# Tile 0 of x goes unscaled into plain fp32 products; its roots multiply the sums, its forms are scaled afterwards

## The chip, the core and the metric

The kernel runs on one core of a Trainium2 chip. Five engines matter here: TensorE (PE in the profile, its weight loads PEld), VectorE (DVE), ScalarE (ACT), GpSimd (POOL), and SyncE (SP), which issues most loads; POOL issues the DMAs that add to what lies at their target. The metric is the time of one execution in microseconds (us), as the median of several runs.

## What is computed

One layer of a hybrid encoder block on x of 1024 tokens by 1024 features. What the change touches is the norm at the start, and the projection of its result by the columns of `w_in` that give `vs`, the input of the gating branch:

```python
def rmsnorm(x, g):
    xf = x.astype(jnp.float32)
    y = xf * lax.rsqrt(jnp.mean(xf * xf, axis=-1, keepdims=True) + EPS)
    return (y * g.astype(jnp.float32)).astype(x.dtype)
...
        h = rmsnorm(x, norm_g[l])
        proj = h @ w_in[l]
        q, k, v, za, u, vs, zs, gm = jnp.split(proj, IN_SPLITS, axis=-1)
```

The root of a token is a factor on its whole row, so it can be multiplied in before the product or after it; g is a factor on each feature and has to be there before. Attention, the other projections, the gating and the final norm follow and are not changed.

## The kernel before, in words

**Products.** A product of 1024x1024 by 1024x1024 is done by 2x2 blocks of 512 in seven block products rather than eight (Strassen's scheme in Winograd's form). The forms of h that go into the seven are named `b11, t1, t2, b21, t3, b22, t4`, those of the weight `a11, s1, s2, a12, s3, s4, a22`. Each operand is split into a high part in fp32r (a cast on ACT) and the rest (a subtraction on DVE), and a block product is three fp32r products: high by high, high by low, low by high. So a tile of 128 tokens costs, for one block product, 4 chunks of 128 features by 3 terms, 12 matmuls of 128x128 by 128x512.

**The first stage** makes `vs`, token tile by token tile, while x is still coming in. SP issues loads of 512 KB in this order: x tile 0, the two halves of a11, x tile 1, the two halves of a12, x tile 2, the two halves of s1's first block, g spread over 128 partitions, x tiles 3 and 4, and, as buffers come free, x tiles 5, 6, 7. For each x tile, `scale_of` (L616) squares and sums the rows on ACT and makes the root in five small steps on DVE and one on ACT; `turned_half` (L626) multiplies half a tile by root and g on DVE (L629) and turns it on PE in four transposes into a PSUM bank named `ps_sc` (L634), of which there are two. Tiles 0 to 3 are the first token half: `first_tile` (L654) makes the high and low parts of b11 and b21 from the banks and keeps the raw values in `xh`, and `first_product` (L763) makes the block products by a11 (`accs[t]`) and by a12 (`m2`, stored in `xh` by ACT). Tiles 4 to 7 are the second token half: `second_tile` (L668) subtracts from the kept raw values of tile t-4, and makes the forms t1 and b22, from the same two banks. `by_s1` and `by_s4` then make the block products of t1 and b22, four tiles each; those of tiles 2 and 3 use the `ps_sc` banks too. The products by s2 on the form t2 follow, and from there on the stage and the rest of the kernel keep their order under the change.

**The order.** The engines' queues are filled at build by a scheduler that goes by its own estimates. `after(second, first)` forbids only that the second comes earlier than the first on its engine; it does not place it. An engine's queue is worked through in the order in which it was filled.

**The start.** Before the first x tile is there, PE multiplies ones by ones (`keep_busy`, 12 matmuls), and g, split in two parts in partition 0 of `g_both`, is spread over the 128 partitions by a product with ones into two banks (`spread`, L573), from which tiles 0 and 1 are scaled.

## Time and profile before

| | us |
|---|---|
| median of 3 runs | 901.23 |
| lowest and highest run | 900.76, 901.72 |
| the profiled execution, whole | 901.17 |
| its span, first to last instruction | 899.4 |
| PE busy in the span | 889.1 |
| granted TensorE clock, mean | 0.998 |

1.77 us of the profiled execution lie outside its span. Times within the trace count from the span's start. In a timeline row stand the start, the length up to the end of the last of the merged instructions, the engine, the line, what it writes and reads, and in square brackets the idle time before it and what ended it. PE's matmuls overlap: one of 512 columns lasts 0.39 us, and the next starts 0.227 us after it. Names lose their numbers in the profile: `ps_sc` is any of the two banks, `wr` any x tile in its landing buffer, `T_t1h` the high part of form t1.

### The profile page before, as it was taken

The page shows a single profiled execution, that of the slowest core. Times are in us where ns is not written, and L with a number is a line of the kernel's source. Part 1 is how long each engine was busy: PE and PEld are TensorE (multiplying, and loading weights), DVE is VectorE, ACT ScalarE, POOL GpSimd, SP SyncE. Part 2 cuts the span into 40 slices and gives each one's busy share as a digit, 9 for nine tenths or more (in the row PEclk, how much of TensorE's full clock was granted, in tenths as well). Part 3 has the DMA queues.
Part 4 walks back from the last instruction along what each step waited for, and adds up shares of the span by engine and source line. Part 5 has one row for each costly group of instructions (what it writes and reads, how often), then busy time and mean ns, then how long its engine had stood idle before and what let it go on. Part 6 is the DMA issues. An engine that isn't in the chain of part 4 may idle for free.

```text
span 899.4 us, 13233 instructions
## 1 busy us (share of the span) xinstructions
PE 889.1 (99%) x4304; PEld 743.7 (83%) x4304; DVE 685.8 (76%) x1251; ACT 532.0 (59%) x1064; POOL 149.8 (17%) x213
## 2 busy tenths in 40 slices
PE   8999999999999999999999999999999999999997
PEld 6788888888888888888888888888888888888885
DVE  7879966666687788888878888646796488479986
ACT  7875533334455567676777776755585376467453
POOL 2322222203030001111210111100121121110012
PEclk9999999999999999999999999999999999999999
DMA  9997888868778767878787788899899789998533
GB/s 327 215 258 218 263 208 175 165 157 260 259 253 284 214 188 213 216 151 214 178 221 227 248 241 194 232 316 365 308 284 376 288 226 259 301 301 282 186 116 118
DMA packets 132750, 213.77 MB, mean 238 GB/s; under 512 B 12777, under 2 KB 61161, under 8 KB 132682
## 3 DMA queue, kind: packets, MB, share of 16 engines
q1 hardware_dynamic: 110072, 149.74, 49.9%
q0 software_dynamic: 22464, 62.93, 31.4%
q8 instruction: 34, 0.56, 0.2%
q14 instruction: 34, 0.28, 0.1%
q10 hardware_dynamic: 146, 0.27, 0.1%
HBM read 147.74 MB, written 86.11 MB: 260 GB/s over the span
## 4 chain that ended last, share of the span: by engine, by line
PE 97%; DMA 1%; ACT 1%; DVE 0%; issue 0%; SPq 0%
PE ps_mm L353 42%; PE ps_o L353 27%; PE ps_tp L353 7%; PE ps_sc L1341 3%; PE ps_sc L353 3%; PE ps_tp L750 2%; PE ps_o L1428 2%; PE ps_tp L1387 2%; PE ps_mm L750 2%; PE ps_o L750 2%; PE ps_tp L1012 2%; PE ps_sc L750 1%; PE ps_sc L634 1%; DMA T_t3h<-in_w_dram 1%; ACT wh L162 0%
## 5 line engine op out<-in xcount | busy, mean ns | idle before, releaser
L162 ACT CAST wh<-s 128x1024 fp32r<-128x1024 f32 (+1 forms) x79 | 79.3, 1006 | 92.8 <-PE ps_mm L353 42.4
L163 DVE TENSOR_TENSOR wl<-wr,wh 128x512 fp32r<-128x512 f32 (+1 forms) x77 | 72.0, 936 | 53.2 <-ACT wh L162 52.6
L163 DVE TENSOR_TENSOR wl<-s,wh 128x1024 fp32r<-128x1024 f32 (+1 forms) x79 | 92.6, 1172 | 11.0 <-ACT wh L162 10.9
L162 ACT CAST wh<-wr 128x512 fp32r<-128x512 f32 (+1 forms) x77 | 63.1, 820 | 59.6 <-PE ps_mm L353 30.5
L353 PE MATMUL ps_o<-T_t1h,wh 128*128 128x512 f32 x148 | 58.6, 396 | 0.0
L353 PE MATMUL ps_o<-T_t1h,wl 128*128 128x512 f32 x148 | 57.7, 390 | 0.0
L353 PE MATMUL ps_o<-T_t1l,wh 128*128 128x512 f32 x148 | 57.6, 389 | 0.0
L1356 ACT ACTIVATE pr<-ps_sc,sm 128x192 f32<-128x192 f32 (+2 forms) x128 | 50.9, 410 | 7.4 <-DVE sm L1350 6.4
L353 PE MATMUL ps_mm<-T_t3h,wh 128*128 128x512 f32 x140 | 54.9, 392 | 0.0
L353 PE MATMUL ps_mm<-T_b11h,wh 128*128 128x512 f32 x140 | 54.9, 392 | 0.0
L353 PE MATMUL ps_mm<-T_b11l,wh 128*128 128x512 f32 x140 | 54.7, 391 | 0.0
L353 PE MATMUL ps_mm<-T_t3h,wl 128*128 128x512 f32 x140 | 54.7, 390 | 0.0
L353 PE MATMUL ps_mm<-T_b11h,wl 128*128 128x512 f32 x140 | 54.7, 390 | 0.0
L353 PE MATMUL ps_mm<-T_t2h,wl 128*128 128x512 f32 x140 | 54.6, 390 | 0.0
L353 PE MATMUL ps_mm<-T_t2h,wh 128*128 128x512 f32 x140 | 54.6, 390 | 0.0
L353 PE MATMUL ps_mm<-T_t2l,wh 128*128 128x512 f32 x140 | 54.5, 390 | 0.0
L353 PE MATMUL ps_mm<-T_t3l,wh 128*128 128x512 f32 x140 | 54.5, 389 | 0.0
L353 PE MATMUL ps_mm<-T_t4h,wh 128*128 128x512 f32 x136 | 53.6, 394 | 0.0
L353 PE MATMUL ps_mm<-T_t4h,wl 128*128 128x512 f32 x136 | 53.2, 391 | 0.0
L353 PE MATMUL ps_mm<-T_t4l,wh 128*128 128x512 f32 x136 | 52.9, 389 | 0.0
L307 POOL DMA_DIRECT2D sums<-in_w_dram x40 | 29.8, 939 | 91.6 <-ACT x L371 42.2
L353 PE MATMUL ps_o<-T_b22h,wh 128*128 128x512 f32 x108 | 42.7, 395 | 0.0
(420 smaller groups left out, 2448.2 us busy)
## 6 DMA issues: line engine op xcount, KB each, us to landing
wr<-in_w_dram SPq DMA_DIRECT2D x86, 256.0 KB
sums<-in_w_dram POOLq DMA_DIRECT2D x20, 512.0 KB, 7.0
s<-sums SPq DMA_DIRECT2D x20, 512.0 KB
q_hl<-qhl SPq DMA_DIRECT2D x16, 512.0 KB
q<-q_hl SPq DMA_DIRECT2D x64, 128.0 KB
y_dr<-x POOLq DMA_DIRECT2D x28, 256.0 KB, 6.7
g<-in_w_dram POOLq DMA_DIRECT2D x12, 512.0 KB, 6.6
wr<-in_w_dram SPq DMA_DIRECT2D x11, 512.0 KB
```

The lines of the kernel that those rows point to most:

```text
L162: hi_of.append(nc.scalar.copy(hi, src))
L163: return nc.vector.tensor_sub(lo, src, hi.bitcast(F32))
L307: return lambda: paced(nc.gpsimd.dma_start(dst, src, accum_op=op))
L353: nc.tensor.matmul(acc, lt, rt, start=fresh and k == 0 and n == 0, stop=k == 3 and n == 2, skip_group_check=True,)
L634: turns.append(nc.tensor.transpose(pt[:, i * P : (i + 1) * P], xt[:, k * P : (k + 1) * P], ident[:]))
L750: mm = nc.tensor.matmul(acc[:], lt, rt, start=fresh and k == 0 and n == 0, stop=k == 3 and n == terms[-1], skip_group_check=True,)
L1012: nc.tensor.matmul(pm[:, t * P : (t + 1) * P], xh[:, half * 4 + t, g * P : (g + 1) * P], bias[-1][1][:, g % 4, :], start=True, stop=True,)
L1341: nc.tensor.matmul(sc[:, i, k0:], q_of[:, c, i * P : (i + 1) * P], kt[:, f, k0:], start=f == 0, stop=f == 1,)
L1356: nc.scalar.activation(held_in[c, i], sc[:, i, lo:hi], AF.Exp, bias=nmax[:, c, i : i + 1], scale=-1.0, accum_out=sums[:, c, i : i + 1],)
L1387: nc.tensor.transpose(dst, pr[:, i, block * P : block * P + width], ident[:])
L1428: nc.tensor.matmul(po[:, cs], lt, rt, start=n == 0, stop=n == len(terms) - 1)
```

## The change

Tile 0 is turned as it lands, without root or g (`turn_unscaled`); DVE multiplies by g on the way from the bank to `xh`, with g as one column for each chunk of features (`g_col`, made by eight turns of one row on PE). Its two block products go as plain fp32 matmuls, unsplit, 4 and 4, straight on the raw weights that have landed (`unscaled_product`); ACT multiplies both sums by the root (the products end in `accs[0]` and `m2` as before). The forms b11 and b21 of tile 0, which later stages need, are made afterwards: the root is put on a diagonal, a product with ones spreads it across (`spread_root`, one fp32 matmul of 128x128 by 128x128), DVE multiplies the raw values by it, and they are split as before (`scale_unscaled`). The keep-busy matmuls go from 12 to 6. The spread of g moves in between the products of tile 0. Tile 1's products take the low part of b11 and b21 last. `amid` asks that the transposes of tiles 2 to 5 come no earlier than a given matmul, and the work of tile 4 stands between the two halves of the split of s1. `after.py` writes lines some 40 to 80 higher: L632 for L634, L645 for L647, L627 for L629, L792 for L750.

```diff
@@ -96,14 +96,18 @@
-    plain = mtile([P, D], F32, "wl", 3)[:, 0:HALF]
     g_row = mtile([P, D], F32, "wh", 3)[0:1, :]
     nc.scalar.dma_start(g_row, norm_g.partition_broadcast(1))
-    nc.vector.memset(plain, 1.0)
+    ones_r = mtile([P, 4, HALF], F32R, "T_b22l", 1)[:, 0, :]
+    g_both = mtile([P, 4, HALF], F32R, "T_t1h", 1)
+    nc.vector.memset(ones_r.bitcast(F32), 1.0)
     ident = const.tile([P, P], F32, name="ident")
...
     nc.gpsimd.memset(eps_sb[:], EPS)
+    g_col = const.tile([P, KC], F32, name="g_col")
+    for at, engine in ((0, nc.vector), (2, nc.gpsimd)):
+        engine.memset(g_both[:, at : at + 2, :].bitcast(F32), 0.0)
     warm = const.tile([P, 1], F32, name="warm")
...
@@ -540,9 +544,6 @@
-    ones_r = slot("b22l", (P, HALF))
-    ones_made = nc.vector.tensor_copy(ones_r[:], plain)
     fed = []
...
@@ -552,15 +553,11 @@
         for _ in range(n):
-            feed(nc.tensor.matmul(idle[:], ones_r[:, 0:P], ones_r[:], start=True, stop=True))
+            feed(nc.tensor.matmul(idle[:], ones_r[:, 0:P], ones_r, start=True, stop=True))
...
     g_in = [bank("tp") for half in range(2)]
-    g_both = slot("t1h")
     g_parts = [g_both[:, 2 * n : 2 * n + 2, :] for n in range(2)]
-    for half in range(2):
-        after(nc.vector.memset(g_parts[0][:, half, :].bitcast(F32), 0.0), ones_made)
-    nc.gpsimd.memset(g_parts[1].bitcast(F32), 0.0)
     for half in range(2):
...
@@ -573,11 +570,12 @@
-    keep_busy(4)
-    for n in range(2):
-        for half in range(2):
-            spread(n, half)
-    keep_busy(8)
+    keep_busy(5)
+    g_turned = bank("o")
+    for k in range(KC):
+        feed(nc.tensor.transpose(g_turned[:, k : k + 1], g_row[:, k * P : (k + 1) * P], ident[0:1, 0:1]))
+    g_kept = nc.scalar.copy(g_col[:], g_turned[:, 0:KC])
+    keep_busy(1)
...
@@ -620,10 +618,10 @@
-            after(square, casts[2 * t - 3])
+            after(square, casts[2 * t - 5])
         return xt, rstd_of(ss[:], 1.0 / D)
...
-    def turned_half(xt, r, j):
+    def turned_half(xt, r, j, t=None):
         cs = half_of(j)
...
@@ -632,8 +630,8 @@
             turns.append(nc.tensor.transpose(pt[:, i * P : (i + 1) * P], xt[:, k * P : (k + 1) * P], ident[:]))
-            if len(turns) == 1:
-                feed(turns[0])
+            if t == 1:
+                feed(turns[-1])
         return pt
...
@@ -651,19 +649,63 @@
-    def first_tile(t, scale=None):
-        xt, r = scale or scale_of(t)
-        left = []
-        for j, name in enumerate(("b11", "b21")):
-            pt = turned_half(xt, r, j)
-            form_of(name, t, by_k(pt[:]))
-            if j:
-                left.append(lambda pt=pt: nc.scalar.mul(raw_b21(t), pt[:], -1.0))
-            else:
-                left.append(lambda pt=pt: nc.scalar.copy(raw_sum(t), pt[:]))
-            if t:
-                left.pop()()
-        return left
+    def first_half(t, j, xt, r):
+        name = ("b11", "b21")[j]
+        pt = turned_half(xt, r, j, t)
+        form_of(name, t, by_k(pt[:]))
+        if j:
+            return lambda: nc.scalar.mul(raw_b21(t), pt[:], -1.0)
+        return lambda: nc.scalar.copy(raw_sum(t), pt[:])
+    def first_tile(t):
+        xt, r = scale_of(t)
+        for j in range(2):
+            first_half(t, j, xt, r)()
+    def unscaled(j):
+        return by_k((raw_sum, raw_b21)[j](0))
+    def turn_unscaled(j):
+        pt = bank("sc")
+        for i in range(4):
+            k = j * 4 + i
+            feed(nc.tensor.transpose(pt[:, i * P : (i + 1) * P], x_in[0][:, k * P : (k + 1) * P], ident[:]))
+        return nc.vector.tensor_mul(
+            unscaled(j), by_k(pt[:]), g_col[:, 4 * j : 4 * j + 4].unsqueeze(2).broadcast_to([P, 4, P])
+        )
+    def unscaled_product(acc, j, *ks):
+        for k in ks:
+            feed(
+                nc.tensor.matmul(
+                    acc[:],
+                    unscaled(j)[:, k, :],
+                    raws[("a11", "a12")[j]][:, k, :],
+                    start=k == 0,
+                    stop=k == 3,
+                    skip_group_check=True,
+                )
+            )
+    def spread_root(r):
+        diagonal, across = (x_place(1, 1, 0)[:, i * P : (i + 1) * P] for i in range(2))
+        nc.scalar.mul(diagonal, ident[:], r[:])
+        summed = bank("sc")[:, 0:P]
+        nc.tensor.matmul(summed, ones_r[:, 0:P].bitcast(F32), diagonal, start=True, stop=True)
+        nc.scalar.copy(across, summed)
+        return across.unsqueeze(1).broadcast_to([P, 4, P])
+    def scale_unscaled(j, across, late=None):
+        hi, lo = (v[:, :, tokens(0)] for v in hb[("b11", "b21")[j]])
+        raw = unscaled(j)
+        if j:
+            after(nc.vector.scalar_tensor_tensor(raw, raw, -1.0, across, op0=ALU.mult, op1=ALU.mult), late)
+        else:
+            nc.vector.tensor_mul(raw, raw, across)
+        split(hi, lo, raw, j == 1)
...
@@ -755,17 +797,27 @@
                     )
+                    steps.append(mm)
         return mm
...
     accs = {}
+    steps = []
     t5s = {}
+    def amid(t, half, product, n):
+        turn, step = turns[8 * (t - 1) + 4 * half], steps[24 * (product - 1) + n]
+        after(turn, step)
...
         accs[t] = bank("mm" if t < 2 else "tp")
-        terms = (0, 1, 2) if t else (0, 2, 1)
-        vs_product(accs[t], "b11", t, "a11", True, terms=terms)
         m2 = bank("o")
-        vs_product(m2, "b21", t, "a12", True, terms=terms)
+        for acc, name, weight in ((accs[t], "b11", "a11"), (m2, "b21", "a12")):
+            if t == 1:
+                vs_product(acc, name, t, weight, True, terms=(0, 1))
+                vs_product(acc, name, t, weight, False, terms=(2,))
+            else:
+                vs_product(acc, name, t, weight, True)
         nc.scalar.copy(x_place(0, 0, t), m2[:])
...
@@ -783,25 +835,28 @@
-    first = scale_of(0)
     for name, at in (("a11", "t3h"), ("a12", "t3l")):
...
     first_lows = []
+    _, root = scale_of(0)
+    after(squares[0], g_kept)
+    turned = [turn_unscaled(j) for j in range(2)]
+    after(of_mean[0], turned[1])
     split_vs(0)
+    after(first_lows[0], turned[1])
+    accs[0] = bank("mm")
+    unscaled_product(accs[0], 0, 0, 1)
+    for n in range(2):
+        for half in range(2):
+            spread(n, half)
+    unscaled_product(accs[0], 0, 2, 3)
+    split_vs(1)
     second = scale_of(1)
-    unsplit = first_tile(0, first)
-    after(of_mean[1], lows[0])
-    after(first_lows[0], scalings[1])
-    after(lows[0], first_lows[0])
-    split_vs(1)
-    after(first_lows[2], lows[0])
-    after(lows[1], first_lows[2])
-    after(casts[0], hi_of[0])
-    after(squares[1], casts[0])
-    after(casts[1], squares[1])
+    after(squares[1], hi_of[0])
+    after(of_mean[1], first_lows[2])
     for c in (2, 3):
...
@@ -814,11 +869,21 @@
         x_in[t] = load_x(t)
-    for c in (2, 3):
-        split_vs(c)
-        after(first_lows[c + 1], lows[1])
-        after(hi_of[c - 1], casts[1])
-    for move in unsplit:
+    m2 = bank("o")
+    split_vs(2)
+    after(hi_of[1], of_root[1])
+    unscaled_product(m2, 1, 0, 1, 2)
+    split_vs(3)
+    left = [first_half(1, 0, *second)]
+    unscaled_product(m2, 1, 3)
+    left.append(first_half(1, 1, *second))
+    after(hi_of[2], hi_of[1])
+    after(first_lows[3], scalings[1])
+    after(first_lows[4], first_lows[3])
+    after(lows[0], first_lows[4])
+    m2_kept = nc.scalar.mul(x_place(0, 0, 0), m2[:], root[:])
+    after(nc.scalar.mul(accs[0][:], accs[0][:], root[:]), casts[1])
+    for move in left:
         move()
...
@@ -827,23 +892,40 @@
     raws["s2"], raws["s4"] = raws["a11"], raws["a12"]
-    first_tile(1, second)
-    after(scalings[2], first_lows[4])
+    first_tile(2)
+    after(of_mean[2], lows[0])
+    after(lows[1], scalings[3])
+    after(squares[2], hi_of[2])
+    after(casts[0], squares[2])
+    after(of_root[2], casts[0])
+    after(casts[1], of_root[2])
+    after(m2_kept, casts[1])
     g_of[:] = [g_sb[:, half, :] for half in range(2)]
-    first_tile(2)
-    first_product(0)
     first_tile(3)
+    after(of_mean[3], lows[1])
     first_product(1)
+    amid(2, 0, 1, 11)
+    amid(2, 1, 1, 15)
+    across = spread_root(root)
+    scale_unscaled(0, across)
     s1_hl = slot("t2h"), slot("t2l")
...
             vs_w["s1", 2 * c + k] = hi[:, k, :], lo[:, k, :]
-    second_tile(4)
+        if c == 0:
+            second_tile(4)
     first_product(2)
+    amid(3, 0, 2, 7)
+    amid(3, 1, 2, 13)
+    scale_unscaled(1, across, lows[-1])
     second_tile(5)
     first_product(3)
+    amid(4, 0, 3, 3)
+    amid(4, 1, 3, 9)
+    amid(5, 0, 3, 17)
+    amid(5, 1, 3, 21)
     for c in range(2):
...
```

What the scheduler makes of it, at three places. First PE's queue at the start, before (`ps_sc_196`, `ps_sc_204`: tile 0 turned; `ps_mm_296`: its product by a11):

```order
L555 MATMUL ps_sc_123<-T_b22l_121 128x512 x8
L634 MATMUL ps_sc_196<-ident,wr_119 128x128 x4
L634 MATMUL ps_sc_204<-ident,wr_119 128x128 x4
L750 MATMUL ps_mm_296<-wh_177,T_b11h_150 128x512 x2
L750 MATMUL ps_mm_296<-wh_177,T_b11l_151 128x512 x2
L750 MATMUL ps_mm_296<-wl_178,T_b11h_150 128x512 x2
L750 MATMUL ps_mm_296<-wh_211,T_b11h_150 128x512 x2
L750 MATMUL ps_mm_296<-wh_211,T_b11l_151 128x512 x2
L750 MATMUL ps_mm_296<-wl_212,T_b11h_150 128x512 x2
```

and in the change (`ps_sc_175`, `ps_sc_181`: tile 0 turned; L682: the fp32 products by a11, `ps_mm_193`, and by a12, `ps_o_235`; L570: the spread of g; `ps_sc_248`, `ps_sc_257`: tile 1 turned):

```order
L673 MATMUL ps_sc_175<-ident,wr_123 128x128 x4
L673 MATMUL ps_sc_181<-ident,wr_123 128x128 x4
L682 MATMUL ps_mm_193<-T_t3h_157,xh_120 128x512 x2
L570 MATMUL ps_tp_126<-T_t1h_69,T_b22l_68 128x512
L570 MATMUL ps_tp_127<-T_t1h_69,T_b22l_68 128x512
L570 MATMUL ps_tp_126<-T_t1h_69,T_b22l_68 128x512
L570 MATMUL ps_tp_127<-T_t1h_69,T_b22l_68 128x512
L682 MATMUL ps_mm_193<-T_t3h_157,xh_120 128x512 x2
L682 MATMUL ps_o_235<-T_t3l_158,xh_120 128x512 x3
L632 MATMUL ps_sc_248<-ident,wr_161 128x128 x4
L682 MATMUL ps_o_235<-T_t3l_158,xh_120 128x512
L632 MATMUL ps_sc_257<-ident,wr_161 128x128 x4
```

Of the 24 matmuls of tile 0 there are 8, they stand behind the loads of the weights and no longer behind splits, and tile 1 is turned among them.

Second, ACT's queue around the square of x tile 3 (`wT,st<-T_t1l`), before:

```order
L663 COPY xh_116<-ps_sc_249 128x512
L661 ACTIVATE xh_116<-ps_sc_258 128x512
L619 ACTIVATE wT_154,st_61_323<-T_t1l_223 128x1024
L647 CAST T_b11h_150<-ps_sc_279 128x4x128
```

and in the change:

```order
L658 COPY xh_120<-ps_sc_248 128x512
L617 ACTIVATE wT_152,st_61_304<-T_t1l_226 128x1024
L657 ACTIVATE xh_120<-ps_sc_257 128x512
L645 CAST T_b11h_148<-ps_sc_287 128x4x128
```

The row L661 (L657), which empties the second bank of tile 1, stood ahead of the square of tile 3 and stands behind it now.

Third, PE's queue where tile 5 is turned (`ps_sc_463`, `ps_sc_473`, then `ps_sc_454`, `ps_sc_464`), and the first products by s1 (`ps_o_517` and `ps_o_508` of tile 4; `ps_o_572` of tile 5). Before:

```order
L750 MATMUL ps_o_495<-wh_232,T_b21l_153 128x512 x2
L634 MATMUL ps_sc_463<-ident,wr_226 128x128 x4
L634 MATMUL ps_sc_473<-ident,wr_226 128x128 x4
L750 MATMUL ps_o_495<-s_236,T_b21h_152 128x512 x2
L750 MATMUL ps_o_495<-s_237,T_b21h_152 128x512 x2
L750 MATMUL ps_o_495<-s_236,T_b21l_153 128x512 x2
L750 MATMUL ps_o_517<-T_t2h_380,T_t1h_398 128x512 x2
L750 MATMUL ps_o_517<-T_t2l_381,T_t1h_398 128x512 x2
L750 MATMUL ps_o_517<-T_t2h_380,T_t1l_399 128x512 x2
L750 MATMUL ps_o_517<-T_t2h_380,T_t1h_398 128x512 x2
L750 MATMUL ps_o_517<-T_t2l_381,T_t1h_398 128x512 x2
L750 MATMUL ps_o_517<-T_t2h_380,T_t1l_399 128x512 x2
```

In the change:

```order
L792 MATMUL ps_o_508<-T_t2l_369,T_t1h_384 128x512 x2
L792 MATMUL ps_o_508<-T_t2h_368,T_t1l_385 128x512 x2
L792 MATMUL ps_o_508<-T_t2h_368,T_t1h_384 128x512 x2
L792 MATMUL ps_o_508<-T_t2l_369,T_t1h_384 128x512 x2
L792 MATMUL ps_o_508<-T_t2h_368,T_t1l_385 128x512 x2
L632 MATMUL ps_sc_454<-ident,wr_229 128x128 x4
L632 MATMUL ps_sc_464<-ident,wr_229 128x128 x4
L792 MATMUL ps_o_572<-T_t2h_368,T_t1h_384 128x512 x2
```

And where tile 7 is turned and the third product by s1 follows, before (`ps_sc_608`, `ps_sc_618`; `ps_sc_663`):

```order
L634 MATMUL ps_sc_608<-ident,wr_230 128x128 x4
L750 MATMUL ps_o_581<-wh_509,T_b22h_400 128x512
L750 MATMUL ps_o_581<-wl_510,T_b22h_400 128x512 x2
L634 MATMUL ps_sc_618<-ident,wr_230 128x128 x4
L750 MATMUL ps_o_581<-wh_509,T_b22l_401 128x512 x2
L750 MATMUL ps_o_581<-wh_513,T_b22h_400 128x512 x2
L750 MATMUL ps_o_581<-wl_514,T_b22h_400 128x512 x2
L750 MATMUL ps_o_581<-wh_513,T_b22l_401 128x512 x2
L750 MATMUL ps_sc_663<-T_t2h_380,T_t1h_398 128x512 x2
```

and in the change (`ps_sc_599`, `ps_sc_609`; `ps_sc_654`):

```order
L792 MATMUL ps_o_572<-wh_504,T_b22l_387 128x512 x2
L632 MATMUL ps_sc_599<-ident,wr_233 128x128 x4
L632 MATMUL ps_sc_609<-ident,wr_233 128x128 x4
L792 MATMUL ps_sc_654<-T_t2h_368,T_t1h_384 128x512 x2
```

The transposes of tile 5 stood 18 matmuls ahead of the end of the first product by s1; they stand behind it now, and the next row is the product that reads tile 5. Those of tile 7 stood 11 and 8 matmuls ahead of the third product by s1, and stand right ahead of it now.

## The prediction

> **What bounds the kernel now.** I read the page first, then the chain that ended last, the waits, and the timelines of PE, ACT and DVE up to 63 us.
>
> ```profile
> span 899.4 us, 13233 instructions
> ...
> PE 889.1 (99%) x4304; PEld 743.7 (83%) x4304; DVE 685.8 (76%) x1251; ACT 532.0 (59%) x1064; POOL 149.8 (17%) x213
> ...
> PE 97%; DMA 1%; ACT 1%; DVE 0%; issue 0%; SPq 0%
> ```
>
> The chain is PE almost from end to end. The busy times by stretch (columns: stretch, its length, then PE, PEld, DVE, ACT and POOL with counts, clock, DMA share, GB/s) say where PE still has room:
>
> ```profile
> 5.60:17.50 11.90, 10.59 (x49) 7.41 (x48) 9.84 (x21) 9.84 (x19) 3.20 (x3) 1.00 1.01 398
> 17.50:62.50 45.00, 44.80 (x216) 35.94 (x217) 36.75 (x77) 33.60 (x63) 12.05 (x14) 1.00 1.04 236
> 62.50:899.40 836.90, 830.28 (x4033) 697.87 (x4031) 635.79 (x1147) 484.82 (x979) 132.82 (x188) 1.00 0.80 236
> ```
>
> And where the chain turns into PE for good:
>
> ```profile
> 1.64 6.55 DMA T_t3h<-in_w_dram
> ...
> 17.53 3.02 PE ps_mm L750 x12
> ...
> 51.79 10.88 PE ps_sc L750 x48
> ```
>
> Until 17.5 us the start runs through a load, splits, a root and scalings; from the first product of tile 1 at 17.53 on PE does not stop. So the change can win only in the first 17.5 us, while whatever it makes PE wait before 62.5 us is added in full: behind that stretch the longest wait of a weight load is 0.4 us, so nothing there takes up a delay.
>
> ```profile
> PEld ps_o L1428 <- DVE x L383: 0.4, 1, 0.4
> ```
>
> **Prices on PE.**
>
> ```profile
> 5.71 2.02 PE L555 MATMUL ps_sc<-T_b22l 128*128 128x512 f32 x8
> 7.75 1.33 PE L634 MATMUL ps_sc<-ident,wr 128*128 128x128 f32 x8
> ...
> 112.41 1.95 PE L1012 MATMUL ps_tp<-wT,xh 128*128 128x128 f32 x16
> 114.11 0.48 PE L353 MATMUL ps_mm<-T_t4h,wh 128*128 128x512 f32 x1
> ...
> L1012 PEld LDWEIGHTS ps_tp<-wT,xh x128: 187/192/192, 112.2 to 187.1; 128*128 128x128 f32 x128
> ```
>
> In the chain 48 fp32r products take 10.88 us: 0.227 each. L1012 is the only plain fp32 product shown: 8 instructions of 128 columns, two records each, hold PE from 112.41 to 114.11 at least and 1.78 at most (16 records of 0.111, the distance of the transposes). That is 0.22 for 128 columns, and four times that, 0.89, for 512. Tile 0 then costs 8 x 0.89 = 7.1 us of PE in place of 24 x 0.227 = 5.4: 1.7 more. An fp32 product of 512 columns is not in the trace; from below it is at least 4 x 0.2125 = 0.85, from above 1.27 if its two weight loads (0.19 each at L1012) stood open. I take 0.89, which scales the row without a gap. The root's product, 128 columns, is 0.22.
>
> **The start, step by step.** Loads land one behind the other, 0.524 MB at 398 GB/s, one in 1.32 us. The third, a11's second half, lands at 1.64 + 6.55 = 8.19. So x tile 1 is there at 9.5, a12 at 10.8 and 12.1, x tile 2 at 13.5, and x tile 3, the eleventh, at 18.7. The eighth should then land at 14.8, and POOL, waiting for it, starts at 14.87:
>
> ```profile
> 14.87 1.04 POOL L606 DMA_DIRECT2D T_t4h<-in_w_dram  x1 [6.34 <-DMA T_t4h<-in_w_dram]
> ...
> 24.60 0.86 POOL L606 DMA_DIRECT2D T_t3h<-T_t4h  x1 [7.58 <-DVE T_t1l L629]
> ...
> 4.50 1.06 ACT L619 ACTIVATE wT<-wr 128x1024 f32<-128x1024 f32 x1 [0.27 <-DMA wr<-in_x_dram]
> ...
> 19.40 1.05 ACT L619 ACTIVATE wT<-T_t1l 128x1024 f32<-128x1024 f32 x1
> 20.35 0.19 ACT L619 ACTIVATION_READ_ACCUMULATOR wT<-T_t1l 128x1 f32 x1
> ```
>
> x tile 0 lands at 4.5. Behind the turns of g and one keep-busy matmul its eight transposes end near 6.3; DVE multiplies both halves by g, 0.6 each, until 7.3, so PE begins the fp32 products at 7.0. Two (1.78), the four spreads (0.91), two more: 11.45. a12 is there by then; three products 14.1, half of tile 1 turned (0.44), the last product 15.45, the other half 15.9. The turns of tile 1 find their data: square at 9.5, root done at 11.9, scaled by 13.3. So the first product of tile 1 starts at **15.9 and not 17.53: 1.6 us won**, the whole of the gain. Splits of a11 and a12, still needed by tiles 1 to 3, lie beside it on ACT and DVE.
>
> **First new wait: x tile 3.** Behind the last turn of tile 1 (15.9 and 0.2 to its end) ACT has a cast, the two multiplications by the root and a copy, 0.49 each, reaches the square of tile 3 at about 18.1 and stands until 18.7, when it lands; before, ACT came there at 19.40 and found it. The square with its read holds ACT about 1.05, and only then L657 empties the bank in which tile 2's second half is to be turned: 18.73 + 1.05 + 0.6 and a step to PE = 20.55. PE is there at 15.9 + 16 x 0.227 + 0.44 = 19.95. **0.6 lost**, and from here PE's place is tied to the landing, whatever the fp32 products took within 0.6.
>
> **Second: tile 5.** From 20.55 to the end of the first product by s1 PE has 68 matmuls, 20 transposes and the root's product: 15.4 + 2.2 + 0.2 = 17.9, so it could be done at 38.4. Next are tile 5's transposes, which need it scaled by DVE.
>
> ```profile
> 29.54 1.22 DVE L652 TENSOR_TENSOR T_t2l<-T_t4h,T_t2h 128x1024 fp32r<-128x1024 f32 x1
> 30.68 0.68 DVE L674 TENSOR_TENSOR xh<-xh,ps_sc 128x512 f32<-128x512 f32 x1
> ...
> 34.83 0.16 DVE L150 TENSOR_TENSOR st<-st,st 128x1 f32<-128x1 f32 x1
> 35.02 1.41 DVE L629 SCALAR_TENSOR_TENSOR wr<-wr,st,xh 128x512 f32<-128x512 f32 x2
> 36.36 0.69 DVE L683 TENSOR_TENSOR xh<-xh,T_t4l 128x512 f32<-128x512 f32 x1
> 36.96 0.68 DVE L674 TENSOR_TENSOR xh<-xh,ps_sc 128x512 f32<-128x512 f32 x1
> ```
>
> From start to start a split of 1024 takes 1.14, a scaling 0.67, a subtraction 0.60, a small step 0.17 to 0.2. In the change tile 4's second half is turned by 32.5 (20.55, then 42 matmuls, 20 transposes and the root's product, 12.0), its cast on ACT done by 33.3, and between there and tile 5's scaling DVE has: two small steps 0.34, a subtraction 0.61, tile 0's multiplication by the root 0.67 (new), a subtraction 0.61, a small step 0.17, a subtraction 0.61, the second split of s1 1.14 (before, it stood far ahead of tile 5), tile 0's split 0.67 (new): 4.8, so 38.15. The scalings end at 38.9 and 39.55, and PE waits 0.4 for the one and 0.2 for the other, and 0.1 before that for the split. The transposes end at 40.07. The next product reads t1 of tile 5, and for this ACT does three things in its queue's order, as it does here for tile 6:
>
> ```profile
> 45.94 0.59 ACT L647 CAST T_b22h<-ps_sc 128x512 fp32r<-128x512 f32 x1 [1.08 <-PE ps_sc L634]
> 46.42 0.61 ACT L675 ACTIVATE x<-ps_sc 128x512 f32<-128x512 f32 x1
> 46.91 0.62 ACT L647 CAST T_t1h<-xh 128x512 fp32r<-128x512 f32 x1
> ```
>
> That is 0.2 to the end of the last transpose, 0.48 + 0.49 + 0.62 and a step: 1.9. Before, 18 matmuls (4.1 us) covered this trip; in the change nothing stands between. **2.6 lost at tile 5.**
>
> **Third: tile 7.** 36 matmuls and 8 transposes later (9.1 us) PE turns tile 7 right ahead of the third product by s1. That product writes the bank of tile 7's first half, so it waits for ACT's cast of the second half and then its copy of the first: 0.2 + 0.48 + 0.6 and a step, 1.36; and tile 7's scaling on DVE, queued behind the late work of tile 6, costs 0.5 more. **1.9 lost.** Before, 8 matmuls and more stood between.
>
> **The sum.** What falls away in turn are the small stalls of before in the same stretch: from 17.53 to
>
> ```profile
> 62.51 0.61 PE L750 MATMUL ps_mm<-wh,T_t2h 128*128 128x512 f32 x2
> ```
>
> are 44.98 us, of which 168 matmuls and 48 transposes make 38.1 + 5.3; 1.5 was waiting. So: -1.6 (start) + 0.6 (tile 3) + 0.2 (root's product) + 2.6 (tile 5) + 0.1 (tile 6) + 1.9 (tile 7) - 1.5 = **+2.3**. The span becomes 901.7; with the 1.77 outside it the profiled execution goes from 901.17 to 903.5, which stands to the median of 901.23 as near as nothing. Forecast **903.5**. Its own bounds: the tile 5 trip can be 0.6 shorter if DVE's scaling is in time, and DVE can be 0.8 later by its order: 902.7 to 904.4. What costs nothing here costs nothing for named reasons: the unsplit products' larger price and ACT's two multiplications by the root are covered by the wait for tile 3; and the doubled reads of a11 and a12 are over by 15.5, ahead of the POOL adds into them, which come from 24.60 on (POOL's second row above).
>
> **Rivals.**
> *The start gain stays* (the other side). If DVE and ACT finish tiles 5 and 7 ahead of PE, only -1.6 + 0.6 + 0.2 is left, and up to 1.5 of the old stalls may go too: 899 to 900.4, say 900. For it speaks that DVE is busy 36.75 of 45 us; against it that the two trips begin with transposes that end where the reader starts. It decides from the point where 4 us of other matmuls stand between, and none do. 9%.
> *One trip only.* If the bank of tile 7 comes free by the other buffer, 1.9 falls away: 901.6. 10%.
> *The clock opens late.* PE's products begin at 2.19 at some 0.45 each:
>
> ```profile
> 2.19 2.08 PE L555 MATMUL ps_sc<-T_b22l 128*128 128x512 f32 x4 [2.19 <-DVE T_b22l L544]
> ```
>
> and run at 0.23 from 5.71, 3.5 us later. The change has half the keep-busy matmuls, with transposes and a gap of 0.6 behind them. If full speed came 3.5 us later, at 9.2, two us of fp32 products would go at half speed and the transposes of tile 0 be later by 0.4: 1.5 more, 1.2 of it behind what the wait for tile 3 hides: 904.7. 13%. [...]
> *Weight loads stand open* in the fp32 products: 8 x 0.38 = 3.0, 0.6 hidden: 905.9. Against it: at L1012 they overlap. 4%.
>
> **How the numbers follow.** The forecast has 64%. A measurement here tells 0.2% from no change: below 899.4 is faster, above 903.03 slower. Of the 64, some 52 lie above 903.03; with the late clock and the open loads 69 slower. Same: 12 of the forecast, 10 for one trip, 5 of the first rival: 27. Faster: 4. The range goes from 901.8 to 905.0: it leaves out the first and the last rival and the edges.
>
> **What would show it.** After: the first product of tile 1 (L792 on `ps_mm`) at 15.9; PE idle by 0.6 near 20, freed by ACT L657; two gaps, of about 1.9 near 42 ahead of `ps_o<-T_t2h`, freed by ACT L645, and of about 1.4 near 54 ahead of `ps_sc<-T_t2h`, freed by ACT L717; the products on form t2 beginning near 64.8 and not 62.5. Wrong, if those gaps are under 1 us; if fp32 matmuls stand more than 1 us apart; or if PE's first products on a11 last twice as long.

## The result: slower, and by four times what was forecast

| | before | after |
|---|---|---|
| median of four runs, us | 901.36 | 910.27 |
| lowest and highest run | 900.76, 901.72 | 909.09, 911.64 |
| ratio, 95% interval | | 1.0100 (1.0088 to 1.0113) |
| profiled execution, whole | 901.17 | 910.05 |
| its span | 899.4 | 908.3 |

The forecast was 903.5 with a range up to 905.0. 8.9 us were added; 2.3 were forecast.

### The profile after

Of the page of the changed kernel, the span and the head of the chain that ended last:

```profile
span 908.3 us, 13224 instructions
...
PE 85%; issue 6%; DVE 3%; DMA 3%; POOL 1%; ACT 1%; POOLq 0%; DVEq 0%; ACTq 0%
```

The chain was 97% PE and is 85% PE: DMA, DVE, POOL and ACT have come into it, so PE waits somewhere where it did not. The waits of PE (line waited for, in total, times, longest) say where:

```profile
PE ps_mm L792 <- ACT wh L166: 3.3, 1, 3.3
PE ps_o L792 <- ACT T_t1h L645: 1.7, 1, 1.7
...
PE ps_sc L792 <- ACT x L717: 1.2, 1, 1.2
```

The second and third were forecast. The first, the longest, was not. PE's timeline puts it behind 70.58:

```profile
65.60 0.62 PE L792 MATMUL ps_mm<-wh,T_t2h 128*128 128x512 f32 x2
...
70.58 0.61 PE L792 MATMUL ps_tp<-wh,T_t2l 128*128 128x512 f32 x2
74.47 0.99 PE L792 MATMUL ps_mm<-wh,T_t2h 128*128 128x512 f32 x2 [3.27 <-ACT wh L166]
75.73 1.22 PE L792 MATMUL ps_mm<-wl,T_t2h 128*128 128x512 f32 x2 [0.27 <-DVE wl L167]
...
79.26 0.61 PE L792 MATMUL ps_tp<-wh,T_t2h 128*128 128x512 f32 x2
```

and the same products before:

```profile
67.94 0.61 PE L750 MATMUL ps_mm<-wh,T_t2h 128*128 128x512 f32 x2
68.40 0.62 PE L750 MATMUL ps_mm<-wl,T_t2h 128*128 128x512 f32 x2
...
70.67 0.61 PE L750 MATMUL ps_tp<-wh,T_t2h 128*128 128x512 f32 x2
```

Read the delay off such pairs. The first product on form t2 comes at 65.60 against 62.51: 3.1 late, near the forecast 2.3. The next pair is 74.47 against 67.94: 6.5. One pair on, 75.73 against 68.40: 7.3, since the low half of the weight is late as well (the row calls only 0.27 of these 0.8 a wait, because the pair ahead took 0.99 and not 0.61). At 79.26 against 70.67 it is 8.6, and the span ends 8.9 late. In the stretch between, the clock had gone down: it reads 0.50 from 75 to 78. The first of these by its row (length, then PE, PEld, DVE, ACT, POOL with counts, granted clock, DMA share, GB/s):

```profile
75.00:76.00 1.00, 0.73 (x3) 0.27 (x2) 0.80 (x2) 1.00 (x2) 0.00 (x0) 0.50 0.21 82
```

So the 8.9 are: 3.1 up to 65.6; 3.4 of standing; 0.8 for the low half; 1.3 at half clock; 0.3 later.

### Behind the stop: a DMA that landed 9.7 us later

PE waited for ACT's cast of the weight s2 (L166). ACT's timeline shows what held ACT, after:

```profile
70.54 0.59 ACT L836 COPY xh<-ps_sc 128x512 f32<-128x512 f32 x1 [6.55 <-DMA xh<-xh]
...
73.39 1.03 ACT L166 CAST wh<-T_t3h 128x1024 fp32r<-128x1024 f32 x1
```

and before:

```profile
60.85 0.59 ACT L784 COPY xh<-ps_sc 128x512 f32<-128x512 f32 x1
...
63.70 1.03 ACT L162 CAST wh<-T_t3h 128x1024 fp32r<-128x1024 f32 x1
```

The copy (`keep_t5`, the third block product by s1 put into `xh`) overwrites what one of POOL's adding DMAs, tile 6's, reads. Before, it stands there without a wait. The DMAs issued in a window of 1 us, with KB and us to landing, give this add before, and after:

```profile
xh<-xh POOLq DMA_DIRECT2D x1, 256.0 KB, 10.1
```

```profile
xh<-xh POOLq DMA_DIRECT2D x1, 256.0 KB, 19.5
```

Of POOL's issues before, those of tile 5's and tile 6's add:

```profile
41.74 0.86 POOL L606 DMA_DIRECT2D xh<-xh  x1 [0.31 <-DVE xh L683]
...
50.67 0.86 POOL L606 DMA_DIRECT2D xh<-xh  x1 [0.38 <-DVE xh L683]
```

Before, tile 6's add was issued at 50.67, so landed near 60.8: ACT's copy started at 60.85 and had at most a tenth of a us to spare. After it was issued at 50.94, hardly later, and landed at 70.44. The chain of waits of the changed kernel leads back from there (start, length, what):

```profile
44.49 2.35 DVE wl L650 x2
46.84 0.61 DVE xh L725
...
47.74 0.86 POOL xh L604
...
50.94 19.50 DMA xh<-xh
```

DVE makes tile 5's sum (L725) behind two splits of s4 now, since tile 5 is turned late; so POOL issues tile 5's add at 47.74 and no longer at 41.74, and behind it in one go two adds of 512 KB and two more of 256 KB. Just then the DMA engines ran nearly empty. The stretch 50 to 54 before, and after:

```profile
50.00:54.00 4.00, 4.00 (x19) 3.30 (x18) 3.77 (x7) 3.02 (x5) 2.01 (x3) 1.00 1.08 283
```

```profile
50.00:54.00 4.00, 3.37 (x18) 2.33 (x16) 3.20 (x8) 0.58 (x2) 2.16 (x3) 1.00 0.28 70
```

Five adds wait and the share of the DMA engines is 0.28 at 70 GB/s, not 1.08 at 283. The queues in this stretch (packets, MB, share) are, after:

```profile
DMA packets 660, 0.28 MB, mean 70 GB/s; under 512 B 574, under 2 KB 574, under 8 KB 660
...
q1 hardware_dynamic: 631, 0.23, 20.8%
q0 software_dynamic: 29, 0.05, 7.1%
```

574 packets under 512 B, nearly all of them in SP's queue, and 29 packets of the adds. By their sizes in the trace 358 of the 574 have 8 bytes, 158 have 32 or 64, and the rest 4. Which loads have such pieces is in the code: of the five small loads that SP issues behind a22, three (`ln_g`, `ln_b`, `b_merge`) fill 32 or 64 bytes of each partition, and the two of `sinks` write 2 floats, 8 bytes, at a time:

```python
    of_head = sinks.rearrange("(c e r) -> e c r", e=2, r=2)
    for e in range(2):
        behind(
            nc.sync.dma_start(
                sink_sb[e * 64 : (e + 1) * 64].rearrange("p (c r) -> p c r", r=2),
                of_head[e].partition_broadcast(64),
            ),
            mm,
        )
```

16 heads make 4 pieces in each of 128 partitions, 512 pieces in all (an expectation below says 64 x 8 for each load; it is 64 x 4). SP issued them at 44.17 after, at 45.45 before.

When the pieces were issued tells little of when they ran. By the packets' sizes they ran from 58 to 66 before, behind large loads, and from 48.7 to 55.4 after. Before, they ran beside adds whose packets were already coming, and there the two queues moved about as many packets each, 334 and 331, at a share of 1.27. The queues from 58 to 61, before:

```profile
q0 software_dynamic: 334, 0.61, 111.4%
q1 hardware_dynamic: 331, 0.01, 15.6%
```

So pieces beside adds need not cost anything. After, most of them ran when the last add's packets were through and those of the adds issued from 47.74 on had not begun. Some of the hole is only that: in the first experiment below, without the small pieces, the adds issued from 47.47 on have 2 packets between 50.5 and 51.5 as well, but large loads fill the engines. From 52 to 54 the adds have 135 packets there and 22 in the change; that is what they lose.

### The profile page after: what moved, and what is told of

It reads as the page before. It is cut to its first block, busy times and chain, and to the rows that moved or that the text cites. A ratio compares the mean times of both kernels' runs of the same rounds, so it can differ in the third digit from the quotient of the medians.

```text
span 908.3 us, 13224 instructions
## 1 busy us (share of the span) xinstructions
PE 893.5 (98%) x4300; PEld 744.3 (82%) x4300; DVE 686.4 (76%) x1251; ACT 531.9 (59%) x1066; POOL 149.5 (16%) x213
## 4 chain that ended last, share of the span: by engine, by line
PE 85%; issue 6%; DVE 3%; DMA 3%; POOL 1%; ACT 1%; POOLq 0%; DVEq 0%; ACTq 0%
PE ps_mm L357 36%; PE ps_o L357 25%; PE ps_tp L357 4%; PE ps_sc L1423 3%; PE ps_sc L357 3%; PE ps_o L1510 2%; PE ps_tp L1469 2%; DMA xh<-xh 2%; PE ps_tp L792 2%; PE ps_mm L792 2%; PE ps_tp L1094 2%; PE ps_o L792 1%; DMA bq<-bq 1%; DVE wl L167 1%; POOL y_dr L512 1%
## 5 line engine op out<-in xcount | busy, mean ns | idle before, releaser
L166 ACT CAST wh<-s 128x1024 fp32r<-128x1024 f32 (+1 forms) x79 | 79.3, 1005 | 90.7 <-PE ps_mm L357 42.6
L166 ACT CAST wh<-wr 128x512 fp32r<-128x512 f32 (+1 forms) x77 | 63.1, 820 | 58.4 <-PE ps_mm L357 30.2
```

What stands on the lines that cost most here:

```text
L166: hi_of.append(nc.scalar.copy(hi, src))
```

## The experiments

All times are medians in us, with the kernel before measured on the same chip in brackets, and the ratio's interval. Two theories of the stop at 71 were put against each other: A, the small pieces hold the adds up; B, tile 5's sum is late, whatever else the DMA engines do. None of the edits leaves out a part of the computation.

### The small loads moved away

The five small loads go behind the last product by s1:

```diff
-    behind(nc.sync.dma_start(lg_sb[:], ln_g), mm)
...
-    by_s1(3)
+    mm = by_s1(3)
+    behind(nc.sync.dma_start(lg_sb[:], ln_g), mm)
...
```

> The changed kernel, in which SP issues the five small loads (ln_g, ln_b, b_merge and the two of sinks) behind the fourth product by s1 instead of behind the first one. In the changed kernel PE stands 3.27 us from 71.2 because ACT's third copy of keep_t5 waits until 70.44 for POOL's adding DMA of tile 6 (issued at 50.94); the DMA engines are busy only a quarter of the time from 50 to 54 us, while those small loads run. Theory A, the small loads hold the DMA engines and the adds behind them: without them the add lands before 65, PE no longer stands at 71, 3.3 + 0.8 + 1.2 us (the stop, the wait for the low half of the split behind it, the slow products behind it) come back: 905 (904.5 to 906). Theory B, the adds are late because POOL issues them late and the large loads beside them take the engines: the landing moves by under 2 us, the time stays at 909 to 911.

905.32 (901.31), ratio 1.0026 to 1.0056: 5 of the 8.9 us are gone. The stretch 50 to 54, the queues in it, and ACT's copy:

```profile
50.00:54.00 4.00, 3.10 (x17) 2.10 (x15) 3.15 (x8) 0.85 (x2) 1.88 (x3) 1.00 1.08 328
```

```profile
q1 hardware_dynamic: 388, 0.99, 65.2%
q0 software_dynamic: 172, 0.32, 43.2%
```

```profile
65.45 0.59 ACT L836 COPY xh<-ps_sc 128x512 f32<-128x512 f32 x1 [1.73 <-DMA xh<-xh]
```

The hole is filled, the adds have six times the packets, the copy waits 1.7 and PE at 71 not at all. The adds are issued as late as in the change (tile 5's at 47.47).

### Only the two loads of sinks, and the first pair of weights instead

The first edit moves only the loop over `of_head` behind the last product by s1. The second leaves the small loads and puts four weight loads that SP issues a little later, for the next stage, behind that product:

```diff
     def copy_to(dst, src):
-        nc.sync.dma_start(dst, src)
+        move = nc.sync.dma_start(dst, src)
+        if len(of_first_pair) < 4:
+            of_first_pair.append(move)
+            behind(move, last_by_s1[0])
```

> The changed kernel with only the two loads of sinks (64 x 8 pieces of 8 bytes each) behind the fourth product by s1; the loads of ln_g, ln_b and b_merge stay where they are. If the pieces of 8 bytes hold the DMA engines from 50 to 54 us, this alone does what the five did: 905.3 (904.5 to 906.5), share of the engines over 0.9 from 50 to 54. If any small load does it: in part, 907 to 909.

> The changed kernel with the four loads of the first pair of weights (1 MB together, SP, issued from 50.28 on) behind the fourth product by s1; the small loads stay. Theory A, the small loads leave the engines empty from 50 to 54 us and hold the adds: the add of tile 5 comes no earlier, those behind it somewhat, since the pair no longer runs beside them (it took a quarter of the engines from 56 on): the add of tile 6 near 66, PE's stop mostly gone or under 1 us: 905.5 to 908. Theory B, the bytes beside the adds: the engines are full of adds from 50 on, landing by 62, no stop: 905.3. If neither: 910.

905.96 (900.96), 1.0036 to 1.0066; and 906.49 (900.96), 1.0043 to 1.0074. The stretch 50 to 54 with sinks late, then with the weights late:

```profile
50.00:54.00 4.00, 4.00 (x23) 3.27 (x21) 3.03 (x9) 0.10 (x1) 1.72 (x2) 1.00 1.10 291
```

```profile
50.00:54.00 4.00, 3.86 (x20) 2.72 (x18) 3.64 (x9) 0.44 (x3) 2.66 (x3) 1.00 0.46 96
```

The two loads alone do what the five did. The 32- and 64-byte pieces stayed where they were: 494 packets under 512 B ran in this stretch, and the share was 1.10. With the weights late the hole stays (0.46), and so does a stop of PE, of 1.0 and 0.5; it is shorter, since tile 6's add lands at 68.7 and not at 70.4; that the adds, once free, share the engines with less is the likely reason, and was not shown.

### Tile 5's sum ahead of the splits of s4

```diff
     last_of_h = raw_t2(5)
+    for low in s4_lows:
+        after(low, t2_sums[-1])
```

> The changed kernel, in which DVE makes tile 5's sum (the one that POOL's add of tile 5 waits for) ahead of the two low halves of s4 instead of behind them. POOL's add is then issued near 45.4 instead of 47.74, and what stands behind it on POOL's queue about 2 us earlier too. Theory B, the late issue is the cause: the add of tile 6 lands 5 us or more earlier than 70.4, the stop at 71 shrinks to under 1 us: 905 to 906.5. Theory A, the small loads hold the adds whenever they come: the add of tile 5 gets through ahead of them, those of the weights and of tile 6 do not; landing near 68, a stop of 1 us or so: 906.5 to 908.5.

905.73 (901.31), 1.0031 to 1.0061. Tile 5's add is issued at 45.18, 2.6 earlier, and the loads of sinks at 44.17 as in the change; there is no hole in 50 to 54 (share 1.19), and the copy is back without a wait:

```profile
64.85 0.60 ACT L842 COPY xh<-ps_sc 128x512 f32<-128x512 f32 x1
```

So neither theory is right alone: to take away either side, the small pieces or the lateness, takes away the stop. The stop takes both.

### ACT's copies behind the splits

If only ACT's queue order carried the add's landing to PE, it should help to let the casts of s2 pass the copies:

```diff
     def keep_t5(t):
-        nc.scalar.copy(x_place(0, 1, t), t5s[t][:])
+        kept = nc.scalar.copy(x_place(0, 1, t), t5s[t][:])
+        if t > 1:
+            after(kept, hi_of[-1])
```

> The changed kernel, in which the third and fourth copy of keep_t5 stand behind the split of s2's second half on ACT. If PE's stop at 71.2 comes only from ACT's queue, where the copy that waits for the add stands ahead of the split, it is gone, although the add still lands near 70: 905 (904.5 to 906), as much as if the add were in time. Rival: the wait moves on to what now stands behind the copies on ACT (the split of s3 and the casts of t3), PE stops 2 us later in the program instead: 907 to 909. If the stop has another cause than this copy: 910.

907.76 (901.31), 1.0052 to 1.0082. The stop at 71 is gone and stands further on, where the next form needs what the copies and adds made:

```profile
78.84 0.70 PE L792 MATMUL ps_mm<-wh,T_t3h 128*128 128x512 f32 x2 [1.56 <-DVE xh L1006]
```

Of the 8.9 us some 2.5 came back: the order behind a late transfer repairs it only in part.

### The same edit on the kernel before

If the pieces are what counts, they must harm the kernel before too, once they meet its adds. Only the two loads of sinks go ahead of SP's loads of a22:

```diff
+    of_head = sinks.rearrange("(c e r) -> e c r", e=2, r=2)
+    for e in range(2):
+        behind(nc.sync.dma_start(...), mm)
     a22 = [raw_tile(), mtile([P, D], F32, "s", 2)]
```

> The kernel before, with the two loads of sinks ahead of SP's loads of a22 instead of behind them, nothing else moved. Theory A, the pieces of 8 bytes hold the DMA engines for some 4 us wherever adds stand behind them: the share of the engines falls near 46 to 52 us, the add of tile 6 lands 3 to 4 us later than 60.75, and ACT's copy, which had 0.1 us to spare, waits for it; PE has 3.2 us of cover, so little or nothing is lost: 901.3 to 903.5. Rival, the hole belongs to the changed kernel's late adds alone: the shares stay near 1, the landing stays within 1 us, 901.3.

905.01 (901.55), 1.0026 to 1.0053: 3.5 us from the place of two loads of 2 KB, in a kernel that is otherwise the one before. By stretch, by wait of PE, and ACT's copy:

```profile
48.00:52.00 4.00, 4.00 (x23) 3.29 (x23) 3.77 (x7) 2.15 (x5) 2.57 (x3) 1.00 0.23 46
...
72.00:73.00 1.00, 1.00 (x3) 0.79 (x3) 1.00 (x3) 1.00 (x3) 0.00 (x0) 0.50 0.67 244
```

```profile
PE ps_mm L750 <- ACT wh L162: 1.0, 1, 1.0
PE ps_mm L750 <- DVE wl L163: 0.5, 1, 0.5
```

```profile
65.03 0.59 ACT L784 COPY xh<-ps_sc 128x512 f32<-128x512 f32 x1 [4.25 <-DMA xh<-xh]
```

The same picture step by step: engines at 0.23, the add 4 us later than near 60.8, the copy, the cast, the low half, half clock. The expectation had the waits and left out the clock, and so was too low.

### An unbroken start

Nine keep-busy products in one piece, the turns of g behind them, none between:

```diff
-    keep_busy(5)
+    keep_busy(9)
...
-    keep_busy(1)
```

> The changed kernel, with nine keep-busy products in one piece ahead of the turns of g in place of five ahead and one behind, and ACT's copy of the turned g behind the square of tile 0. In the changed kernel PE works from 1.46 on without a gap, but products run at 0.43 and transposes of x at 0.21 until 9.9 us. Theory, the eight transposes of one row break up the warm-up: now full speed comes near 5.5, the transposes of x tile 0 stand 0.11 apart, the fp32 products 0.86 from the first on, and the first product of tile 1 comes near 16.4 instead of 17.30; behind it DVE's queue ahead of tile 5 takes most of that back: 909.5 (908.8 to 910.3). Rival, full speed comes late whatever runs first: the products of tile 0 begin 0.4 later and are as slow as now, the first product of tile 1 at 17.7: 910.3 to 911.

907.39 (901.31), 1.0054 to 1.0099, with runs from 904.4 to 910.3. The profiled execution was the fastest of them; PE's start in it, and the start of the change for comparison:

```profile
5.92 1.09 PE L671 MATMUL ps_sc<-ident,wr 128*128 128x128 f32 x8
7.43 1.98 PE L680 MATMUL ps_mm<-T_t3h,xh 128*128 128x512 f32 x4 [0.41 <-DVE xh L672]
...
10.18 1.88 PE L680 MATMUL ps_mm<-T_t3h,xh 128*128 128x512 f32 x4
...
16.12 0.71 PE L790 MATMUL ps_mm<-wh,T_b11h 128*128 128x512 f32 x2
```

```profile
5.42 1.91 PE L673 MATMUL ps_sc<-ident,wr 128*128 128x128 f32 x8
7.33 3.25 PE L682 MATMUL ps_mm<-T_t3h,xh 128*128 128x512 f32 x4
...
11.35 1.88 PE L682 MATMUL ps_mm<-T_t3h,xh 128*128 128x512 f32 x4
13.07 2.74 PE L682 MATMUL ps_o<-T_t3l,xh 128*128 128x512 f32 x6
15.64 0.60 PE L632 MATMUL ps_sc<-ident,wr 128*128 128x128 f32 x4
...
17.30 0.71 PE L792 MATMUL ps_mm<-wh,T_b11h 128*128 128x512 f32 x2
```

Each fp32 product has two records. At full clock two of them take 1.72 (11.35 to 13.07) and three 2.57 (13.07 to 15.64). The first two and the spread of g behind them hold PE from 7.33 to 11.35 in the change, 4.02, and with the unbroken start from 7.43 to 10.18, 2.75: in the change the clock opened only in between. With the unbroken start it was open already at tile 0's transposes (1.09 for eight, not 1.91), and the first product of tile 1 came at 16.12, 1.2 earlier. What it won was lost again behind the pause at tile 5, where the clock now closed (0.50 from 43 to 46). The stop at 71 was absent in this execution, though both its sides were there: tile 5's add was issued at 46.56, 1.2 earlier than in the change, the 8-byte pieces ran beside the adds (899 packets of SP's queue and 241 of the adds from 50 to 54, share 1.00), and ACT's copy started at 66.33. So pieces and late adds do not make the stop in every case.

### ACT's order at tiles 5 and 7, and the start with it

On top of the first experiment, ACT and DVE make form t1 of tile 5 ahead of b22, and take the bank's copy ahead of the cast:

```diff
+        if t in (5, 7):
+            after(casts[-1], kept)
+        if t == 5:
+            after(casts[-1], casts[-2])
+            after(lows[-1], lows[-2])
```

> The kernel with the small loads late (905.3), in which ACT makes the negated copy and, at tile 5, the cast of t1 ahead of the cast of b22 at tiles 5 and 7 (and DVE the low half of t1 ahead of that of b22 at tile 5). If PE's two pauses, 1.7 us behind tile 5's turns and 1.2 behind tile 7's, are ACT's order as the prediction said (cast of b22, copy, cast of t1, one behind the other), the first shrinks by one cast and its wait to about 0.8, the second by 0.5 to about 0.7: 904.0 (903.3 to 904.7). Rival, DVE sets the pauses (it was busy 9.2 of 10 us there): they stay, or what DVE does later for tile 6 makes new ones: 905.3 to 906.5.

> The kernel e5_act_order with the unbroken warm-up of e4. The first product of tile 1 near 16.1, 1.2 us earlier than without; with both pauses short the granted clock should stay at 1.00 near 43 to 46 us (in e4 it went to 0.50 there behind the pause of 1.7 us, and took back the 1.2 us): 902.8 (901.8 to 904), still not under the kernel before by more than a measurement can tell. Rival, DVE's queue ahead of tile 5 takes the 1.2 us back, or the clock closes again: 904 to 905.

904.65 (900.96), 1.0027 to 1.0057; and with the unbroken start too 904.72, 1.0023 to 1.0052. The first lies inside its range, the second above it. PE's two pauses fell from 1.7 to 1.2 and from 1.2 to none, but PE now comes earlier to the casts of s2, which still wait for the add (65.4), and loses 0.3 and 0.5 there. And with the same nine products as in the last experiment the clock opened only at the end of the first two fp32 products:

```profile
1.45 4.21 PE L556 MATMUL ps_sc<-T_b22l 128*128 128x512 f32 x9 [1.45 <-DVE T_b22l L103]
...
6.53 1.97 PE L671 MATMUL ps_sc<-ident,wr 128*128 128x128 f32 x8
...
18.43 0.70 PE L795 MATMUL ps_mm<-wh,T_b11h 128*128 128x512 f32 x2
```

2.3 us later than the 16.12 of the same start. More keep-busy products do not buy the clock reliably: with these nine it opened at 5.0 and at 11.1.

### All mends together

The small loads late, ACT's order, and the sum ahead of the splits:

> The kernel e5_act_order (small loads late, ACT's order at tiles 5 and 7) with DVE making tile 5's sum ahead of the low halves of s4, as in e3. In e5 PE was only 1.1 us behind the kernel before at 61 us, and lost 1.4 again at 69.5 since ACT's third copy waited for the add until 65.4; in e3 the add landed at 60.8. If that tie is all, the copy no longer waits, and the 1.1 us stay: 902.8 (902 to 903.6), not faster than before, since the start gains only 0.2 to 0.3 with the clock opening near 10 us. Rival, the late low halves of s4 make PE wait at the products by s4 instead (in e3 the clock closed for 2.5 us after the first pause): 904 to 905.5.

903.89 (901.55), 1.0017 to 1.0042, the best of this family, a little above the range and still slower than before. Pauses of 1.2 at tile 5 and 0.7 at tile 7 are left, and 0.3 for a low half of s4; the copy waited 1.7 for the add, and PE for nothing there.

### Tile 0's forms on POOL

On top of the first experiment, POOL multiplies tile 0's first half by the root and makes its low part, to free DVE ahead of tile 5; in the second kernel with POOL's two operations ahead of its adds into a12:

```diff
-            nc.vector.tensor_mul(raw, raw, across)
+            nc.gpsimd.tensor_tensor(raw, raw, across, op=ALU.mult)
...
+            low = nc.gpsimd.tensor_tensor(lo, raw, hi.bitcast(F32), op=ALU.subtract)
+            for add in last_adds:
+                after(add, low)
```

> The kernel with the small loads late (905.3), in which POOL instead of DVE multiplies the first half of tile 0 by the root and makes its low half (two operations of 128x512, POOL took 1.27 us for such a one, DVE 0.67); tile 5's scaling then stands about 1.3 us earlier in DVE's queue. If DVE's queue is what puts tile 5's turns right ahead of the product that needs them, they come before the first product by s1 again, as in the kernel before, whose matmuls cover the way over ACT: the pause of 1.7 us falls to under 0.5, PE is some 1.5 us behind the kernel before at 61 us instead of 2.8: 903.7 (902.8 to 904.5). Rival, the pause stays behind the second half's turns, which ACT casts first: 905 to 905.8.

> The kernel e12, with POOL's two operations for tile 0 ahead of its two adds into a12 instead of behind them: in e12 they began only at 35.75, when those adds had been issued, and ACT's cast behind them stopped ACT and then PE for 6.2 us. POOL stands idle from 29.6 to 32.4 in the changed kernel, so they can run from about 30.1 and end near 33.6, where tile 4's subtraction on DVE needs them. If DVE's queue is what puts tile 5's turns right ahead of the product that needs them: its scaling ends 1.3 us earlier, the first half is turned ahead of the first product by s1, the pause of 1.7 us falls to under 0.8: 904.0 (903 to 904.8). Rival, the second half's turns and ACT's cast of them still stand ahead of the cast that PE needs, or POOL's 3.5 us hold up tile 4: 905 to 906.5.

912.62 (901.13), 1.0110 to 1.0144; and 906.13 (901.21), 1.0030 to 1.0063: both misses. In the first, POOL's work stood behind adds that wait for other DMAs, and PE for the whole of it:

```profile
41.35 0.87 PE L632 MATMUL ps_sc<-ident,wr 128*128 128x128 f32 x3 [6.22 <-ACT T_t1h L645]
```

In the second it came in time, and tile 5's halves were turned at 36.73 and 41.42 among other products, and the pause of 1.7 ahead of the product that reads form t1 is gone. That bears out that DVE's queue made tile 5 late. But new waits of 0.9, 0.5 and 0.4 at the turns, and a stretch of half clock between 55 and 58, came in its place.

## Why the prediction was wrong, and where it was right

**The price of the products: right.** 0.89 was taken for an fp32 product of 512 columns; 0.86 was measured at full clock (2.57 for three). The weight loads lie beside them, so that rival falls.

**The start: mis-sized, -1.6 forecast, -0.2 measured.** The first product of tile 1 came at 17.30 and not 15.9. This is the rival that the clock opens late, which had 13%: the first two fp32 products and the spread took 4.0 and not 2.7, 1.3 more. The column of the granted clock reads 1.00 there as before, because it counts as full what lies ahead of the first record of the clock; that first record, the opening, stands at 9.92 in the trace of the change and at 5.62 before. Why the change's clock was late was not shown. In the ten executions with the change's start the clock opened between 8.3 and 11.3, in the two with the start of before at 5.6 and 6.3; but with nine products in a row and no transpose among them it opened at 5.0 once and at 11.1 once.

**The wait for x tile 3: did not come**, since PE arrived later than forecast: 0.6 forecast, nothing measured. With the start, 2.3 + 1.4 - 0.6 = 3.1, and 3.1 is what the products on form t2 were late.

**Tiles 5 and 7: the gaps right, the total in part by luck.** 1.9 ahead of `ps_o`, freed by ACT L645, and 1.4 ahead of `ps_sc`, freed by ACT L717, were forecast as gaps: 1.7 and 1.2 came, freed by those lines; the waits that were forecast at the transposes themselves are not long enough to be listed. From the first product of tile 1 to the first on form t2 it was to be 48.9 with the wait for tile 3, 48.3 without, and it is 48.3. Two errors cancel in this: PE was idle for 3.0 of the 48.3 (busy for 45.33), where waits of 4.6 were forecast; and the 1.5 us of small stalls that were to fall away were no stalls (before, PE was busy for 44.81 of the 44.98), and stayed.

**The step that failed** is this: "whatever it makes PE wait before 62.5 us is added in full: behind that stretch the longest wait of a weight load is 0.4 us, so nothing there takes up a delay". That nothing takes up a delay was right; the sum also used that nothing adds to one, and this the quoted row can't show. An instruction that doesn't wait may have been in time by 10 us or by a tenth. ACT's third copy was in time by a tenth. The sum followed DVE's late sum of tile 5 no further than PE; its other reader, POOL's add, was left out. The add met the 8-byte pieces and landed 9.7 us later. Of these, 0.1 was to spare before the copy, 3.1 was PE's own delay and 3.2 the cover between the end of the cast and PE's need of it (63.70 and 1.03, 67.94): 3.3 to 3.4 of standing is left, and 3.4 was measured, with 0.8 for the low half and 1.3 of half clock behind it.

Three experiments carry this. With either the small pieces (905.3) or the lateness (905.7) taken away the stop is gone; the profiled execution of the first, 904.2, lies 3.0 above that of the kernel before, and 2.8 of it stand already at the first product on form t2 (65.32 against 62.51). Its median lies 4.0 above; where the slower executions lose the rest is not on record. In the kernel before, the place of the pieces alone makes the stop (905.0).

**What stays open.** Why some 500 pieces of 8 bytes leave 16 engines at a fifth to a quarter of their time for 4 us while 1.75 MB of adds wait is not shown. The traces show an order: where the adds' queue had run out of packets while the pieces ran, the next adds started slowly, until the pieces were through (the change, with 22 packets of the adds from 52 to 54, and 105 from 56 to 58, behind the pieces; the copies behind the splits, the first pair late, the kernel before with sinks first); where the packets of one add followed those of the last without a break, adds and pieces went on side by side (before, 334 and 331 packets from 58 to 61; the sum ahead of the splits, the unbroken start). That this decides it is read off seven traces and was not tested. Why the clock opens when it does was not settled either. The traces show that its records lie a whole number of steps of 3.413 us apart within one execution (in the change the clock stayed open for 64.853, 19 steps, and then closed for one; before it stayed open for 890.879, 261 steps). Where the steps fall differs between the executions: the first record stands at 9.92 in the change and at 5.62 before, 1.26 steps apart. Whether these steps set when the clock can open was not tested.

## What to carry to other kernels

When an edit makes an engine later, follow every reader of what it makes, the DMAs first, and ask of each next wait not whether it is zero but by how much it is: issue time and time to landing of the transfer against the start of its reader. Look in the profile for loads made of tiny pieces, 8 bytes here, and keep them away from adding DMAs that are on the path, above all from where the adds' queue runs empty: two loads of 2 KB cost 3.5 us in the kernel before. Beside adds that were already running the same pieces cost nothing that these runs show, and neither did pieces of 32 and 64 bytes with sinks late. And two turns that end right where the reader begins cost their whole trip over ACT and DVE, 1.7 us at tile 5 and 1.2 at tile 7 here; work between them is what hides it.

## What was not expected of the hardware

- Pieces of 8 bytes in SP's queue while POOL's adds are about to start: 631 packets against 29, the engines at 0.28; without the pieces 388 against 172 at 1.08; and with the pieces beside adds that were already running 331 against 334 at 1.27.
- A pause of PE of 1.7 us went with a closing of the clock in three of seven executions. Behind tile 5 it stayed open in the change and in three experiments with that pause (small loads late, first pair late, copies behind the splits); in the unbroken start, with sinks late and with the sum ahead of the splits it went to 0.50 for 3.4 us. From the first product by s1 to the first on form t2 these three take 29.9 to 30.0 us and the other four 28.7, so closing costs 1.2 to 1.3. In the kernel before with sinks first it read 0.50 from 72 to 74, behind two waits of 1.0 and 0.5. In the step of 3.413 us with the pause, PE was busy for 1.64 to 1.66 where the clock closed and for 1.71 to 2.01 where it stayed open, but for 1.91 with sinks first, where it closed: the busy time of the step alone does not tell the two apart.
- The first product of tile 1 came between 16.1 and 18.4 in kernels with nearly the same start, mostly by when the clock opened; these 2.3 us are more than the 1.6 that the start was to win.
